# Splitting x itself for the first two pairs of weight units, and a re-planned order of taps, in a convolution and retention trunk

## The chip, the cores and the metric

One NeuronCore of a Trainium2 chip runs the whole program. Its engines work side by side, each through its own list of instructions in order: TensorE (PE, matrix products), VectorE (DVE), ScalarE (ACT), GpSimd (POOL) and SyncE (SP, which here only starts transfers). They wait for each other through semaphores. The metric is device time in microseconds (us), lower is better. A difference is called faster or slower here when it is over 0.2%, which is 1.6 us.

## The reference

Two layers over x (512 tokens by 1024), each `x <- x + Mixer(RMSNorm(x))`, and a last norm. The change lies in the first layer, a causal convolution module:

```
h = x * rsqrt(mean(x*x) + eps) * g             # per token
a, b, z = split(h @ w_in, 3)                   # 2048 columns each
u = a * sigmoid(b)
c = causal depthwise conv of u, 31 taps, + bias
mu, var = mean and variance of c over the 2048 channels
cn = (c - mu) * rsqrt(var + eps) * ln_g + ln_b
y = silu(cn) * silu(z)
x = x + y @ w_out
```

The second layer is chunked retention with its own projections. The change does not touch it.

## The kernel before, in words

x lies transposed in SBUF as 8 tiles of 128 model channels by 512 tokens. Channels of the projection are on partitions, so a per-token factor has to be a full 128x512 tile.

**Products.** A matrix product in full float32 precision is built from three faster fp32r products: each operand is split into a high part (rounded to fp32r) and a low part (the rest), and `mm3` (lines 231 to 235) adds high by high, high by low and low by high. A *unit* is 128 output columns of the weights, that is 8 blocks of k, 24 products of 128x512. Units 0 to 31 are the pairs (a_j, b_j) for j = 0 to 15, units 32 to 47 are z, and the output projection starts with unit 48. `wpack[p]` holds units 2p and 2p+1 and is loaded by SP (`load`, line 166) into a ring "raw" of two buffers. From pair 3 on, ACT casts the high part (`pos_hi`, line 202) and writes the negated high part into the low buffer (`neg_hi`, line 198), and a GpSimd DMA adds raw to it in place (`dma_lo`, line 206). Pairs 1 and 2 are split by an ACT cast (line 687) and a GpSimd subtraction (line 689).

**The head.** Pair 0 is done in the PE's slow float32 mode, straight from the loaded weights (line 328). The operand is `xg = x*g`, not yet normalised. Squares of x (line 295) are summed over channels by `token_sums` (line 288), `rsqrt` runs 11 tiny DVE operations, and `bcast_mm` (line 273) spreads the factor over the partitions as R1 in PSUM. Then for each k, `h_tile` (line 674) writes xg*R1 to PSUM, ACT casts it to the high part (line 675) and `h_lo` (line 678) makes the low part. Units 2 and 3 (lines 736, 737, 742) and all later units read these.

**The taps.** The 31 taps of each of 16 tiles u_j are shared out. DVE accumulates most of them in PSUM, one tap an instruction (line 521). ACT multiplies some into an SBUF tile (line 436), which GpSimd adds up (line 299). Some pairs of products are added by a GpSimd DMA. A planner with a clock per engine (`it`, a cost for each operation) chooses at build time what stands next on each engine: `fill` looks at what each engine could do, `pool_tile` picks the tile of the next ACT product, and `begin`, `ready` and `conv_op` run the DVE side. Tiles in `APART` keep the DVE sum and the GpSimd sum apart until a last addition (line 500). The others hand the GpSimd sum to DVE first.

**The statistics.** The LN sums run on PE: mu from the first four c tiles, `dsum` sums of c minus that mean, `st` sums of squares. Squares are added in pairs by a GpSimd DMA into `qsum` (line 625). While the last sums come in, PE works on `HOLD` z units that were kept back. Between the sums stand threes of their products. Then a factor `delta` and the new rsqrt `rs` are spread by line 273, LN is applied, and the output projection begins (line 957).

Of the kernel before, what the change touches and what calls it, by code (L numbers as in the profile page):

```python
# [45 lines left out]
SUMLATE = 1.0  # L46
# [4 lines left out]
SUMS_AT = 7  # L51
BCAST_AT = 10
# [45 lines left out]
def trunk(ctx: ExitStack, tc: tile.TileContext, xT, pos, wpack, conv_par, norms, freq, decay, out):  # L98
# [44 lines left out]
    raw0 = ring.tile([P, KD, 2, P], F32, tag="wlo", bufs=3, name="raw0")  # L143
    w0 = wpack[0].rearrange("p a (b c d) -> p (a b) c d", c=2, d=P)
    x_sb = [G() for _ in range(KD)]
    for k in range(0, KD, 2):
        (nc.scalar if k < 4 else nc.sync).dma_start(out=raw0[:, k:k + 2], in_=w0[:, k:k + 2])
        if k < 4:
            for i in range(4):
                nc.sync.dma_start(out=x_sb[2 * k + i], in_=xT[:, 2 * k + i, :])  # L150
# [163 lines left out]
    xg, sq = [], []  # L314
    pa, pb = MM(), MM()
    r1 = R1 = None
# [8 lines left out]
    nc.scalar.activation(sp.tile([P, 1], F32, name="tbl"), nrm[:, 0, 0:1], AF.Sigmoid)  # L325
    for i in range(2 * KD):
        k, c = divmod(i, 2)
        nc.tensor.matmul((pa, pb)[c], raw0[:, k, c, :], xg[k], start=k == 0, stop=k == KD - 1)  # L328
        if i == SUMS_AT:
            r1 = rsqrt(token_sums([sq[0]]), 1.0 / 1024.0)  # L330
        if i == BCAST_AT:
            R1, R1_sb = ST(), G()
            bcast_mm(r1, R1)
            nc.scalar.copy(R1_sb, R1)
    it.now = [21.7, 17.2, 17.2, 17.2, 21.0]
    it.done["R1"] = 17.2
    it.done["pab"] = 21.7
# [357 lines left out]
    h_tile(0)  # L695
    pair = split_pair(1, 17.5)
    next(pair)
    h_tile(1)
    h_lo(0)
    next(pair)  # L700
    h_tile(2)
    h_lo(1)
    list(pair)
    load(3)
    pair = split_pair(2, 21.4)
    it.run(DVE_, 0.66, lambda: nc.vector.tensor_tensor(out=sg0, in0=pb, in1=R1_sb, op=ALU.mult), "bR", ["pab"])
    it.run(ACT_, 0.52, lambda: nc.scalar.activation(sg0, sg0, AF.Sigmoid), "sg", ["bR"])
    h_lo(2)
    h_tile(3)
    it.run(DVE_, 0.66, lambda: nc.vector.tensor_tensor(out=sg0, in0=sg0, in1=R1, op=ALU.mult), "sR0", ["sg"])  # L710
    it.run(DVE_, 0.66, lambda: nc.vector.tensor_tensor(out=u0[:, PADW:], in0=pa, in1=sg0, op=ALU.mult), "u0", ["sR0"])
    u_sb[0] = u0
    h_lo(3)
    next(pair)
    h_tile(4)
    first_tap(0)
    next(pair)
    h_tile(5)
    h_lo(4)
    list(pair)  # L720
    h_tile(6)
    h_lo(5)
    h_tile(7)
    h_lo(6)
    h_lo(7)
    it.now[ACT_] = max(it.now[ACT_], 31.5)
    neg_hi(3)
    dma_lo(3)
    load(4)
# [85 lines left out]
    whi(48)  # L815
# [40 lines left out]
    whi(49)  # L856
    wlo(48, nc.gpsimd)
# [459 lines left out]
```

## Time and profile before

| what | value |
|---|---|
| median of 3 runs | 804.29 us (804.20 to 805.13) |
| the profiled execution, its own time | 804.36 us |
| its span in the profile | 802.4 us |
| PE busy | 98% of the span |
| DVE busy | 72% |
| ACT, POOL busy | 53%, 46% |
| unit 4, the first product of the normal rhythm | starts at 41.25 us |
| spread of `delta` on PE | starts at 289.94 us |

The profiled execution is 0.07 us above the median of the runs, and 1.96 us of its time lie around the span. Times in the profile are counted from the start of the span. A busy PE is not a PE at its peak: its clock can be granted at half.

### The profile page before, as it was taken

The numbers are of one execution on the slowest core, as the hardware profiler recorded it, in microseconds if no ns is written. First come the engines' busy times: TensorE is split into PE (matmuls) and PEld (weight loads), VectorE is DVE, ScalarE is ACT, GpSimd is POOL, SyncE is SP. The second block draws the span as 40 slices with busy tenths as digits, with TensorE's granted clock in tenths as the row PEclk, the third lists the DMA queues.
The fourth block names the chain that finished last, engine by engine and source line by source line (L and its number), as shares of the span: only waits on it lengthen the run. The fifth ranks groups of instructions, "written<-read, shape, count | busy, mean of one in ns | idle before, by whom it ended". The sixth has DMA issues, their size and how long they took to land.

```text
span 802.4 us, 9733 instructions
## 1 busy us (share of the span) xinstructions
PE 789.1 (98%) x3681; PEld 651.7 (81%) x3681; DVE 576.8 (72%) x855; ACT 422.2 (53%) x561; POOL 365.8 (46%) x286
## 2 busy tenths in 40 slices
PE   8999999999999999999999999999999999999995
PEld 3588888888888888888888888888888888888895
DVE  4899999999999948899574576486586467542434
ACT  3589889888998727543233413423424424332421
POOL 0578999989999848720330322340340120000300
PEclk9999999999999999999999999999999999999998
DMA  7367857897798734433213212112122212222103
GB/s 276 124 174 176 210 164 167 211 238 176 199 232 214 182 108 145 171 105 106 105 54 128 81 53 105 53 54 105 52 69 96 99 53 105 105 105 105 53 1 105
DMA packets 18958, 101.58 MB, mean 127 GB/s; under 512 B 2272, under 2 KB 4320, under 8 KB 8032
## 3 DMA queue, kind: packets, MB, share of 16 engines
q1 hardware_dynamic: 14448, 74.73, 26.6%
q0 software_dynamic: 4032, 25.69, 15.8%
q8 instruction: 29, 0.48, 0.2%
q10 hardware_dynamic: 432, 0.54, 0.2%
q14 instruction: 17, 0.14, 0.0%
HBM read 73.17 MB, written 2.10 MB: 94 GB/s over the span
## 4 chain that ended last, share of the span: by engine, by line
PE 95%; DVE 2%; DMA 2%; ACT 1%; issue 0%; SPq 0%; DVEq 0%; ACTq 0%
PE mm L233 28%; PE mm L235 27%; PE mm L234 27%; PE mm L959 2%; PE mm L957 2%; PE mm L958 2%; DMA g<-xT 1%; PE dsum L288 1%; PE mm L328 1%; PE st L288 1%; PE acc L235 1%; PE acc L234 1%; PE acc L233 1%; PE mm L742 0%; PE st L647 0%; DMA nrm<-norms 0%
## 5 line engine op out<-in xcount | busy, mean ns | idle before, releaser
L233 PE MATMUL mm<-g,whi 128*128 128x512 f32 (+1 forms) x832 | 319.8, 385 | 0.0
L234 PE MATMUL mm<-g,whi 128*128 128x512 f32 (+1 forms) x832 | 317.5, 382 | 0.0
L235 PE MATMUL mm<-g,wlo 128*128 128x512 f32 (+1 forms) x832 | 316.8, 381 | 0.0
L521 DVE SCALAR_TENSOR_TENSOR acc<-u,cpar,acc 128x512 f32<-128x512 f32 x324 | 220.8, 753 | 4.7 <-ACT acc L473 3.0
L299 POOL TENSOR_TENSOR accp<-accp,prod 128x512 f32<-128x512 f32 x142 | 190.6, 1383 | 17.2 <-ACT prod L436 10.7
L233 PEld LDWEIGHTS mm<-g,whi 128*128 128x128 f32 x832 | 156.5, 188 | 30.3 <-issue 0.7
L234 PEld LDWEIGHTS mm<-g,whi 128*128 128x128 f32 x832 | 156.5, 188 | 30.1 <-issue 1.0
L235 PEld LDWEIGHTS mm<-g,wlo 128*128 128x128 f32 x832 | 156.4, 188 | 29.9
L187 ACT CAST whi<-raw 128x1024 fp32r<-128x1024 f32 x80 | 80.7, 1050 | 111.3 <-PE mm L234 69.2
L192 DVE TENSOR_TENSOR wlo<-raw,whi 128x1024 fp32r<-128x1024 f32 x70 | 94.5, 1384 | 41.3 <-ACT whi L187 41.3
L299 POOL TENSOR_TENSOR g<-g,g 128x512 f32<-128x512 f32 x23 | 35.5, 1544 | 179.9 <-ACT g L295 171.4
L436 ACT ACTIVATE prod<-u,cpar 128x512 f32<-128x512 f32 x142 | 97.3, 719 | 20.1 <-POOL accp L299 20.0
L1045 POOL TENSOR_TENSOR g<-g,g 128x512 f32<-128x512 f32 x8 | 10.4, 1294 | 142.7 <-DVE g L1043 142.7
L228 DVE TENSOR_TENSOR g<-g,g 128x512 fp32r<-128x512 f32 x36 | 29.0, 820 | 35.7 <-ACT g L227 32.2
L227 ACT CAST g<-g 128x512 fp32r<-128x512 f32 x36 | 22.4, 623 | 60.0 <-POOL g L1045 27.8
L234 PE MATMUL mm<-wlo,g 128*128 128x512 f32 x128 | 49.8, 389 | 0.0
L235 PE MATMUL mm<-whi,g 128*128 128x512 f32 x128 | 49.6, 389 | 0.0
L233 PE MATMUL mm<-whi,g 128*128 128x512 f32 x128 | 49.3, 389 | 0.0
L198 ACT ACTIVATE wlo<-raw 128x2048 fp32r<-128x2048 f32 x21 | 40.1, 1909 | 0.0
L202 ACT CAST whi<-raw 128x2048 fp32r<-128x2048 f32 x21 | 40.0, 1904 | 0.0
L1112 POOL TENSOR_TENSOR o<-o,g 128x512 f32<-128x512 f32 x16 | 27.5, 1747 | 18.2 <-DVE g L267 18.2
L192 POOL TENSOR_TENSOR wlo<-raw,whi 128x1024 fp32r<-128x1024 f32 x10 | 24.3, 2428 | 14.9 <-ACT whi L187 14.9
(207 smaller groups left out, 960.9 us busy)
## 6 DMA issues: line engine op xcount, KB each, us to landing
raw<-wpack SPq DMA_DIRECT2D x63, 1024.0 KB, 4.8
wlo<-raw POOLq DMA_DIRECT2D x21, 1024.0 KB, 8.2
g<-xT SPq DMA_DIRECT2D x16, 256.0 KB, 6.3
q<-q POOLq DMA_DIRECT2D x6, 512.0 KB, 8.0
out_dram<-xo SPq DMA_DIRECT2D x6, 256.0 KB, 2.5
dec<-decay SPq DMA_DIRECT2D x1, 1280.0 KB, 7.5
raw<-wpack ACTq DMA_DIRECT2D x2, 256.0 KB, 5.5
raw<-wpack SPq DMA_DIRECT2D x2, 256.0 KB, 5.6
```

What stands on the lines that cost most here:

```text
L187: it.run(ACT_, 0.95, lambda: nc.scalar.copy(his[p][:, i, :], raws[p][:, i, :]), f"whi{n}")
L192: it.run(e, c, lambda: eng.tensor_tensor(out=lo, in0=raws[n // 2][:, n % 2, :], in1=hi.bitcast(F32), op=ALU.subtract), f"wlo{n}", [f"whi{n}"])
L198: it.run(ACT_, 1.8, lambda: nc.scalar.activation(los[p], raws[p], AF.Copy, scale=-1.0), f"wneg{p}")
L202: it.run(ACT_, 1.8, lambda: nc.scalar.copy(his[p], raws[p]), f"whi{p}", deps)
L228: (eng or nc.vector).tensor_tensor(out=lo, in0=src, in1=hi.bitcast(F32), op=ALU.subtract)
L233: nc.tensor.matmul(o, a[0], b[0], start=first, stop=False)
L234: nc.tensor.matmul(o, a[0], b[1], start=False, stop=False)
L235: nc.tensor.matmul(o, a[1], b[0], start=False, stop=last)
L299: eng.tensor_tensor(out=a, in0=a, in1=b, op=ALU.add)
L436: at = it.run(ACT_, 0.61, lambda: nc.scalar.activation(p, u_sb[j][:, w:w + S], AF.Copy, scale=cpar[:, j, w:w + 1]), at=add_end[n_prod[0]])
L521: it.run(DVE_, cost, lambda: nc.vector.scalar_tensor_tensor(out=c_sb[j] if last else acc, in0=u_sb[j][:, w:w + S], scalar=cpar[:, j, w:w + 1],
L1112: nc.gpsimd.tensor_tensor(out=t, in0=t, in1=RO, op=ALU.mult)
```

## The change

Pair 0 is no longer computed in float32. x*g is split into xh (ACT, line 326 of the changed kernel) and xl (DVE), raw0 into hi0 (ACT, line 330) and lo0 (DVE), and pair 0 becomes 48 products of `mm3`. Units 2 and 3 use the same xh and xl, so they no longer read R1; their u tile is multiplied with R1 afterwards, twice (bR1, sR1). R1 is spread after the first 12 products of units 2 and 3. h for unit 4 on is made from x, g and R1 in one DVE operation into PSUM. A one-element GpSimd copy named "after" reads r1, so that GpSimd's subtractions for pairs 1 and 2 stand behind it. Four products and three GpSimd additions of tile 0 are written by hand between the h tiles. In the planner, some constants change: three units are held, sums are placed with a margin of 1.5 us behind the time that the planner has for their operand, u_0 is no longer apart, pairs of tiles 4, 5 and 6 (j = 8 to 13) are added by DMA in place of 2 to 5, and the weights of the output projection are split behind the last statistics.

```diff
-PAIRS = (2, 3, 4, 5)
+PAIRS = (4, 5, 6)
-APART = (0, 1) + tuple(range(SPLIT, KI))
-POOL_CAP = 16
-LEAD = 8
-RATE = 1.6
+APART = (1,) + tuple(range(SPLIT, KI))
+POOL_CAP = 13
+LEAD = 10
+RATE = 1.69
-HOLD = 2
+HOLD = 3
-SUMLATE = 1.0
+SUMLATE = 1.5
...
-    raw0 = ring.tile([P, KD, 2, P], F32, tag="wlo", bufs=3, name="raw0")
+    raw0, hi0, lo0 = [ring.tile([P, KD, 2, P], dt, tag=tag, bufs=n, name=tag + "0")
+                      for tag, dt, n in (("raw", F32, 2), ("whi", F32R, 2), ("wlo", F32R, 3))]
...
+    def pair0(k):
+        for c, o in enumerate((pa, pb)):
+            mm3(o, (hi0[:, k, c, :], lo0[:, k, c, :]), xs[k], k == 0, k == KD - 1)
...
     for k in range(KD):
-        t = G()
-        nc.vector.tensor_scalar(out=t, in0=x_sb[k], scalar1=nrm[:, 0, k:k + 1], scalar2=None, op0=ALU.mult)
-        xg.append(t)
-        sq.append(square(x_sb[k]))
+        xh, xl = G(F32R), G(F32R)
+        g = nrm[:, 0, k:k + 1]
+        nc.scalar.activation(xh, x_sb[k], AF.Copy, scale=g)
+        if k == 0:
+            sq.append(square(x_sb[0]))
+        elif k % 2:
+            nc.scalar.copy(hi0[:, k - 1:k + 1], raw0[:, k - 1:k + 1])
+        nc.vector.scalar_tensor_tensor(out=xl, in0=x_sb[k], scalar=g, in1=xh.bitcast(F32), op0=ALU.mult,
+                                       op1=ALU.subtract)
+        if k % 2:
+            nc.vector.tensor_tensor(out=lo0[:, k - 1:k + 1], in0=raw0[:, k - 1:k + 1],
+                                    in1=hi0[:, k - 1:k + 1].bitcast(F32), op=ALU.subtract)
+        xs.append((xh, xl))
         if k:
+            sq.append(square(x_sb[k]))
             tadd(nc.vector, sq[0], sq[k])
...
+        if k % 2:
+            pair0(k - 1)
+            pair0(k)
+        if k == 1:
+            keep_warm(4)
+    token_sums([sq[0]], o_st)
+    r1 = rsqrt(o_st, 1.0 / 1024.0)
+    nc.gpsimd.tensor_copy(sp.tile([P, 1], F32, name="after"), r1[:, 0:1])
...
-        if j:
+        if j == 1:
+            it.run(DVE_, 0.66, lambda: nc.vector.tensor_tensor(out=sg, in0=pb, in1=R1_sb, op=ALU.mult), "bR1", ["mm3"])
+            it.run(ACT_, 0.5, lambda: nc.scalar.activation(sg, sg, AF.Sigmoid), "sg1", ["bR1"])
+            fill(it.done["sg1"])
+            it.run(DVE_, 0.66, lambda: nc.vector.tensor_tensor(out=sg, in0=sg, in1=R1, op=ALU.mult), "sR1", ["sg1"])
...
-        it.run(DVE_, 0.64, lambda: nc.vector.tensor_tensor(out=h_ps[k], in0=xg[k], in1=R1, op=ALU.mult), f"h{k}", ["R1"])
+        it.run(DVE_, 0.64, lambda: nc.vector.scalar_tensor_tensor(
+            out=h_ps[k], in0=x_sb[k], scalar=nrm[:, 0, k:k + 1], in1=R1, op0=ALU.mult, op1=ALU.mult), f"h{k}", ["R1"])
...
+                nc.tensor.matmul(os_[c], a, xs[k][0], start=k == 0, stop=False)
+                nc.tensor.matmul(os_[c], a, xs[k][1], start=False, stop=False)
...
+        if k == 2:
+            it.run(PE_, 0.95, lambda: bcast_mm(r1, R1), "R1", at=21.8)
```

On PE, at the end of pair 0, the order before is this (`g` under L736 is h, split; `st` under L273 is R1):

```order
L273 MATMUL st_223<-ident,rs_207 128x128 x4
L328 MATMUL mm_150<-g_175,raw_87 128x512
L328 MATMUL mm_149<-g_180,raw_87 128x512
L328 MATMUL mm_150<-g_180,raw_87 128x512
L328 MATMUL mm_149<-g_185,raw_87 128x512
L328 MATMUL mm_150<-g_185,raw_87 128x512
L736 MATMUL mm_236<-g_239,whi_244 128x512
```

and that of the changed kernel is this, at the same place (`g` under L721 is xh, under L722 xl):

```order
L235 MATMUL mm_154<-g_251,wlo_89 128x512
L288 MATMUL st_155<-ones_118,g_159 128x1 x4
L721 MATMUL mm_294<-g_156,whi_299 128x512
L722 MATMUL mm_294<-g_157,whi_299 128x512
L721 MATMUL mm_295<-g_156,whi_299 128x512
L722 MATMUL mm_295<-g_157,whi_299 128x512
```

Before, R1 was spread in the middle of pair 0 and the products of units 2 and 3 read its h. Now the sums stand behind all of pair 0, the products of units 2 and 3 follow at once, and the spread stands 12 products later.

On ACT, around the end of the h tiles, the order before is this (L675 is the high part of h, L198 the negated high part of pair 3's weights, `wlo_307`):

```order
L381 ACTIVATE accp_283<-u_124,cpar 128x512
L687 CAST whi_275<-raw_137 128x1024
L675 CAST g_287<-mm_289 128x512
L675 CAST g_294<-acc_296 128x512
L675 CAST g_300<-acc_302 128x512
L198 ACTIVATE wlo_307<-raw_262 128x2048
L661 ACTIVATE sg_360<-mm_237 128x512
L436 ACTIVATE prod_372<-u_124,cpar 128x512
```

In the changed kernel it is this (L692 is the high part of h, L448 a product of tile 0, L673 the sigmoid for u_1):

```order
L448 ACTIVATE prod_398<-u_128,cpar 128x512
L692 CAST g_400<-acc_402 128x512
L448 ACTIVATE prod_405<-u_128,cpar 128x512
L692 CAST g_408<-mm_410 128x512
L448 ACTIVATE prod_414<-u_128,cpar 128x512
L692 CAST g_416<-acc_418 128x512
L692 CAST g_422<-acc_424 128x512
L198 ACTIVATE wlo_431<-raw_305 128x2048
L673 ACTIVATE sg_439<-sg_439 128x512
```

Pair 3's negated high part stands behind the last h tile in both, but four products of tile 0 now stand between the h tiles.

On PE, at the last statistics, the order before ends like this (`q_1198` is qsum, `q_2516` the last two squares, L273 the spread of delta):

```order
L235 MATMUL mm_2561<-g_239,wlo_2417 128x512
L288 MATMUL st_1143<-ones_114,q_1198 128x1 x4
L233 MATMUL mm_2561<-g_247,whi_2471 128x512
L234 MATMUL mm_2561<-g_248,whi_2471 128x512
L235 MATMUL mm_2561<-g_247,wlo_2417 128x512
L288 MATMUL st_1143<-ones_114,q_1198 128x1 x4
L233 MATMUL mm_2561<-g_255,whi_2471 128x512
L234 MATMUL mm_2561<-g_256,whi_2471 128x512
L235 MATMUL mm_2561<-g_255,wlo_2417 128x512
L288 MATMUL st_1143<-ones_114,q_2516 128x1 x8
L273 MATMUL acc_2604<-ident,delta 128x128 x4
```

and that of the changed kernel like this (`q_1335` is qsum, `q_2592` the squares of the last two tiles, `g_2545` the last c):

```order
L288 MATMUL st_1181<-ones_118,q_1335 128x1 x4
L233 MATMUL mm_2552<-g_422,whi_2393 128x512
L234 MATMUL mm_2552<-g_423,whi_2393 128x512
L235 MATMUL mm_2552<-g_422,wlo_2346 128x512
L288 MATMUL st_1181<-ones_118,q_1335 128x1 x4
L233 MATMUL mm_2553<-g_360,whi_2499 128x512
L234 MATMUL mm_2553<-g_361,whi_2499 128x512
L235 MATMUL mm_2553<-g_360,wlo_2444 128x512
L288 MATMUL st_1181<-ones_118,q_2592 128x1 x4
L288 MATMUL dsum_1182<-ones_118,g_2545 128x1 x4
L273 MATMUL acc_2657<-ident,delta 128x128 x4
```

The sum of the last c now stands last, directly ahead of the spread of delta, and before the spread six fewer products of held units stand in the program (they stand behind it).

## Rows read from the trace of the kernel before

**Rows 1.** The page: the chain that ended last, share of the span by engine.

```profile
PE 95%; DVE 2%; DMA 2%; ACT 1%; issue 0%; SPq 0%; DVEq 0%; ACTq 0%
```

**Rows 2.** The chain of waits, 0 to 42 us: start, duration, what.

```profile
14.65 1.02 PE st L288 x8
15.67 4.38 PE mm L328 x6
20.05 0.89 PE st L273 x8
...
37.60 3.65 PE mm L742 x16
41.25 0.23 PE mm L233
```

**Rows 3.** Windows: us, then PE, PEld, DVE, ACT, POOL busy, PEclk, DMA share, GB/s.

```profile
12.83:14.62 1.79, 0.00 (x0) 0.00 (x1) 1.67 (x4) 1.20 (x2) 0.00 (x0) 1.00 0.96 387
...
15.50:19.60 4.10, 4.10 (x8) 1.80 (x8) 1.81 (x11) 0.00 (x0) 0.00 (x0) 0.58 0.56 236
...
24.60:33.20 8.60, 6.80 (x23) 3.71 (x21) 7.47 (x13) 6.58 (x10) 7.65 (x4) 1.00 0.35 122
33.20:36.60 3.40, 3.38 (x8) 2.73 (x9) 3.22 (x5) 2.40 (x2) 1.30 (x2) 0.50 0.31 75
...
35.03:279.46 244.43, 244.43 (x1111) 202.15 (x1110) 239.11 (x358) 210.82 (x260) 221.84 (x182) 1.00 0.79 197
```

**Rows 4.** Timelines of ACT, DVE and POOL, 7 to 42 us.

```profile
8.09 0.63 ACT L295 ACTIVATE g<-g 128x512 f32<-128x512 f32 x1 [2.29 <-DMA g<-xT]
9.15 3.38 ACT L295 ACTIVATE g<-g 128x512 f32<-128x512 f32 x5 [0.43 <-DMA g<-xT]
...
34.28 1.92 ACT L198 ACTIVATE wlo<-raw 128x2048 fp32r<-128x2048 f32 x1
...
17.70 0.16 DVE L267 SCALAR_TENSOR_TENSOR rs<-rs,rs 128x4 f32<-128x4 f32 x1
...
33.67 1.44 DVE L678 TENSOR_TENSOR g<-acc,g 128x512 fp32r<-128x512 f32 x2
...
35.89 6.30 DVE L521 SCALAR_TENSOR_TENSOR acc<-u,cpar,acc 128x512 f32<-128x512 f32 x8
...
23.95 7.26 POOL L689 TENSOR_TENSOR wlo<-raw,whi 128x1024 fp32r<-128x1024 f32 x3 [21.45 <-ACT whi L687]
...
36.52 1.01 POOL L206 DMA_DIRECT2D wlo<-raw  x1 [2.10 <-ACT wlo L198]
```

**Rows 5.** DMA landings: L206 all 21, L206's first, L625's last.

```profile
DMA to landing us min/median/max: 6.9/8.2/11.5
...
DMA to landing us min/median/max: 9.0/9.0/9.0
...
DMA to landing us min/median/max: 8.1/8.1/8.1
```

**Rows 6.** Groups by line: count, busy us, mean ns, idle before.

```profile
L521 DVE SCALAR_TENSOR_TENSOR acc<-u,cpar,acc 128x512 f32<-128x512 f32 x324 | 220.8, 753 | 4.7 <-ACT acc L473 3.0
L299 POOL TENSOR_TENSOR accp<-accp,prod 128x512 f32<-128x512 f32 x142 | 190.6, 1383 | 17.2 <-ACT prod L436 10.7
...
L975 DVE SCALAR_TENSOR_TENSOR g<-g,nrm,g 128x512 fp32r<-128x512 f32 x8 | 11.0, 1395 | 0.0
```

**Rows 7.** Timelines of DVE, POOL and PE, 267 to 290 us.

```profile
267.32 2.72 DVE L521 SCALAR_TENSOR_TENSOR acc<-u,cpar,acc 128x512 f32<-128x512 f32 x4
...
278.77 0.69 DVE L500 TENSOR_TENSOR g<-accp,acc 128x512 f32<-128x512 f32 x1 [0.18 <-POOL accp L299]
...
276.54 0.87 POOL L625 DMA_DIRECT2D q<-q  x1
...
285.04 0.95 PE L288 MATMUL st<-ones,q 128*128 128x1 f32 x8
...
289.94 1.14 PE L273 MATMUL acc<-ident,delta 128*128 128x128 f32 x8
```

More of the change, by code (lines that the diff above doesn't have):

```diff
@@ L147, in trunk @@
         (nc.scalar if k < 4 else nc.sync).dma_start(out=raw0[:, k:k + 2], in_=w0[:, k:k + 2])
-        if k < 4:
-            for i in range(4):
-                nc.sync.dma_start(out=x_sb[2 * k + i], in_=xT[:, 2 * k + i, :])
+        for i in range(2):
+            nc.sync.dma_start(out=x_sb[k + i], in_=xT[:, k + i, :])
+    nc.scalar.activation(sp.tile([P, 1], F32, name="tbl"), wz[:, 0:1], AF.Sigmoid)
     cpar = const.tile([P, KI, W + 3], F32, name="cpar")
@@ L313, in trunk @@
         nc.gpsimd.memset(u[:, 0:PADW], 0.0)
-    xg, sq = [], []
+    xs, sq = [], []
     pa, pb = MM(), MM()
-    r1 = R1 = None
+    o_st = ST(NT)
+    def pair0(k):
+        for c, o in enumerate((pa, pb)):
+            mm3(o, (hi0[:, k, c, :], lo0[:, k, c, :]), xs[k], k == 0, k == KD - 1)
     for k in range(KD):
-        t = G()
-        nc.vector.tensor_scalar(out=t, in0=x_sb[k], scalar1=nrm[:, 0, k:k + 1], scalar2=None, op0=ALU.mult)
-        xg.append(t)
-        sq.append(square(x_sb[k]))
+        xh, xl = G(F32R), G(F32R)
[11 more added lines that the diff above has]
+        xs.append((xh, xl))
         if k:
+            sq.append(square(x_sb[k]))
             tadd(nc.vector, sq[0], sq[k])
[L325 to L337, printed above, removed]
+        if k % 2:
[6 more added lines that the diff above has]
+    nc.gpsimd.tensor_copy(sp.tile([P, 1], F32, name="after"), r1[:, 0:1])
+    it.now = [19.6, 16.7, 21.7, 21.9, 20.0]
+    it.done["pab"] = 18.6
     c_sb = [None] * KI
@@ L442, in pool_add @@
         j, p, at = adds.popleft()
-        cost = 1.42 if acc_at[j] == it.now[POOL_] else 1.32
+        cost = 1.48 if acc_at[j] == it.now[POOL_] else 1.38
         acc_at[j] = it.run(POOL_, cost, lambda: tadd(nc.gpsimd, acc_sb[j], p), at=max(at, acc_at[j]))
@@ L694, in trunk @@
     u0, sg0 = u_ring[0], cp.tile([P, S], F32, tag="sg", bufs=1, name="sg0")
[L695 to L703, printed above, removed]
-    load(3)
[L705 to L729, printed above, removed]
+    R1, R1_sb = ST(), G()
+    list(split_pair(1, 16.7))
+    load(3)
     ws = [unit(n) for n in (2, 3)]
@@ L735, in hi_mms @@
             def hi_mms():
-                nc.tensor.matmul(os_[c], a, h_s[k][0], start=k == 0, stop=False)
-                nc.tensor.matmul(os_[c], a, h_s[k][1], start=False, stop=False)
-            it.run(PE_, 0.45, hi_mms, None, [f"hl{k}"])
+                nc.tensor.matmul(os_[c], a, xs[k][0], start=k == 0, stop=False)
+                nc.tensor.matmul(os_[c], a, xs[k][1], start=False, stop=False)
+            it.run(PE_, 0.45, hi_mms, None, ["whi1"])
+        if k == 2:
+            it.run(PE_, 0.95, lambda: bcast_mm(r1, R1), "R1", at=21.8)
     for k in range(KD):
         for c in range(2):
-            it.run(PE_, 0.227, lambda: nc.tensor.matmul(os_[c], ws[c][1][:, k * P:(k + 1) * P], h_s[k][0], start=False,
+            it.run(PE_, 0.227, lambda: nc.tensor.matmul(os_[c], ws[c][1][:, k * P:(k + 1) * P], xs[k][0], start=False,
                                                        stop=k == KD - 1), f"mm{2 + c}", ["wlo1"])
+    it.run(ACT_, 0.52, lambda: nc.scalar.copy(R1_sb, R1), "R1_sb", ["R1"])
+    h_tile(0)
+    pair = split_pair(2, 20.5)
+    next(pair)
+    it.run(DVE_, 0.66, lambda: nc.vector.tensor_tensor(out=sg0, in0=pb, in1=R1_sb, op=ALU.mult), "bR", ["pab", "R1_sb"])
+    it.run(ACT_, 0.52, lambda: nc.scalar.activation(sg0, sg0, AF.Sigmoid), "sg", ["bR"])
+    h_tile(1)
+    it.run(DVE_, 0.66, lambda: nc.vector.tensor_tensor(out=sg0, in0=sg0, in1=R1, op=ALU.mult), "sR0", ["sg"])
+    it.run(DVE_, 0.66, lambda: nc.vector.tensor_tensor(out=u0[:, PADW:], in0=pa, in1=sg0, op=ALU.mult), "u0", ["sR0"])
+    u_sb[0] = u0
+    next(pair)
+    first_tap(0)
+    product(0)
+    h_lo(0)
+    h_tile(2)
+    list(pair)
+    h_lo(1)
+    pool_add()
+    h_tile(3)
+    h_lo(2)
+    product(0)
+    h_tile(4)
+    product(0)
+    h_lo(3)
+    h_tile(5)
+    h_lo(4)
+    product(0)
+    h_tile(6)
+    h_lo(5)
+    h_tile(7)
+    pool_add()
+    pool_add()
+    h_lo(6)
+    h_lo(7)
+    it.now[ACT_] = max(it.now[ACT_], 27.0)
+    neg_hi(3)
+    fill(it.done["wneg3"])
+    dma_lo(3)
+    load(4)
+    it.now[PE_] = max(it.now[PE_], it.done["hl7"] - 4.7)
     def unit_mm(n):
```

14 lines of the change are left out of this document (6 added, 8 removed).

## The prediction

> **What bounds the kernel now.** I read the chain of waits first. 95% of the span is PE [rows 1], so time can only be won where PE waits, works at half clock, or does work that the change removes. I then looked for such places from the start. PE does pair 0 in slow float32, with the token sums in the middle of it, and unit 4 begins at 41.25 us [rows 2]. The windows show two half-clock stretches in that head: 15.5 to 19.6 us has a granted clock of 0.58, right after PE stood idle from 12.83 to 14.62, and 33.2 to 36.6 us has 0.50, after a stretch in which PE was busy for 6.8 of 8.6 us [rows 3]. From 35 to 279 us PE is busy all the time at full clock [rows 3]. So the head can be shortened, and whatever is won there is kept only if nothing later makes PE wait.
>
> Two things later could. One is DVE: from 35.03 to 279.46 us it is busy for 239.1 of 244.4 us [rows 3], and the last statistics hang on its last c, which ends at 279.46 [rows 7]. The other is the first low part made by DMA (pair 3): its transfer is issued at 36.52 and lands 9.0 us later [rows 4, 5], at 45.5. Unit 6 reads it with its third product. A product takes 3.65/16 = 0.228 us [rows 2], so that is 41.25 + 50 x 0.228 = 52.65: 7.1 us to spare before.
>
> **The head, step by step.** x's third tile is there at 8.1 [rows 4]; x and raw0 come in another order, but no tile later than the squares need. ACT then has 15 operations for k = 2 to 7 (6 xh, 6 squares, 3 casts). Five squares took 3.38 us, waits for x included [rows 4], so at most 0.68 each; I take 0.57, an estimate, which ends at 16.7. DVE has 15 too (6 xl, 3 lo0, 6 additions) and starts at about 8.9, behind the first xh of these. xl is not in the trace. The nearest operation is the tap, 0.66 us from one to the next (2.72 us for four, the last 0.75 long) [rows 7]; a two-input subtraction takes 0.72 at most [rows 4]. The same form with SBUF inputs and GpSimd at work takes 1.395 [rows 6]. GpSimd rests here, so I take 0.62, with bounds 0.58 and 1.395. The last lo0 is the 14th: 8.9 + 14 x 0.62 = 17.6. PE then has 10 products left, 2.3 us, and ends pair 0 at 19.9.
>
> Then the sums, 1.0 us [rows 2], to 20.9. rsqrt took from 15.67 to 17.86 [rows 2, 4], 2.2 us, so r1 is there at 23.1. PE fills that time with 12 products of units 2 and 3, to 23.7, and spreads R1 in 0.9 [rows 2]: **R1 at 24.6, against 20.94 before, 3.7 later.** GpSimd's rest costs nothing: its subtractions start at 23.1 in place of 23.95, at 2.4 us each [rows 4], and pair 1's low part is there at 28, ahead of its first use at 24.6 + 20 x 0.228 = 29.2. Units 2 and 3 end 36 products after the spread, at 32.8.
>
> The eight h tiles take as long as before: from R1 to the end of the last low part 35.11 - 20.94 = 14.2 us [rows 2, 4], so 38.8. h now reads x and R1 in one operation, which saves xg (8 operations) and adds nothing here; the four products between the h tiles lie in ACT's idle time. PE is through units 2 and 3 by 32.8, so unit 4 follows the low parts and ends one block after the last, at about 39.3. Unit 5 ends at 44.8, and unit 6's third product comes at 45.3.
>
> **What is late next: pair 3's low part.** Its negation stands on ACT behind the last h tile, as before, and R1 is 3.7 later. From R1 to the DMA's issue it was 36.52 - 20.94 = 15.6 us [rows 2, 4], so the issue comes at 40.2. The 21 transfers of this kind take 6.9 to 11.5 us, the first 9.0 [rows 5]. That first one ran beside the load of pair 4, which starts when GpSimd has split pair 2. In the changed kernel GpSimd ends that at about 33, and the load is over by 40, so I take the lower bound: 47.1, with 49.2 above. PE waits 1.8 us there. By the Trainium skill ("DMA: Bandwidth & Descriptors", section on the SWDGE path) a transfer on this path costs about 2.0 us plus its bytes at 436 GB/s, which is an estimate of 4.4 us for 1 MB. The trace disagrees: none of 21 took less than 6.9 us [rows 5].
>
> So at unit 6's third product PE leads by 52.65 - 47.1 = 5.5 us. An idle 1.79 us stood before the first half-clock stretch of the trace [rows 3], and the wait here is as long, so I count on a third such stretch: 3.4 us at 0.50 [rows 3] loses 1.7. **The lead is then 3.8 us.** The skill's page "TensorE: Matmul & The Clock Gate" (section on HAM oscillation) shows a kernel whose waits between bursts of products bring the lower rate each time. By that the 1.7 is lost, without it the lead is 5.5.
>
> **The tail.** DVE starts its taps later: R1 + 14.2, and then u_1 needs a product with R1, a sigmoid behind pair 3's negation, another product and u itself, 2.8 us: 41.6 in place of 35.03. But it has less to do. In the two orders I count 3 taps fewer (2.3 us at 0.753 [rows 6]), 17 fewer taps directly behind one of the same sum (0.79 from one to the next within such a row [rows 4], 0.66 in alternation [rows 7], so 2.2 us), one last addition and one u tile fewer (0.7 each). That is 5.8, so 239.1 - 5.8 = 233.3 us of work. It waited 5.3 us in that stretch before. GpSimd now starts adding within the head and has 9 additions fewer (12 us [rows 6]) for 6 more short DMA issues, so I take 3.5, with 2 and 5.3 as bounds. **The last c ends at 41.6 + 233.3 + 3.5 = 278.4** (276.9 to 280.2), against 279.46.
>
> The last DMA of squares stands ahead of five GpSimd additions of 1.38 us [rows 6], so it is issued 8.2 to 9.5 us before the last c and lands 8.1 later [rows 5], 0.1 to 1.4 us before it. From the first sum that reads it to the spread of delta it was 289.94 - 285.04 = 4.9 us [rows 7]; the new order has the same pieces there. So DVE and the DMA allow the spread at 278.4 + 3.7 to 5.0 = 282.1 to 283.4. PE gets there by its own work at 289.94 - 3.8 - 1.4 = 284.7, where 1.4 is the six products that now stand behind the spread, so that the time is not won by them. PE is the later one, so the whole lead arrives. Behind the spread PE has 36 products in place of 30 to cover the rsqrt and the LN, and the moved casts and subtractions of the output weights (2.4 us each on GpSimd [rows 4]) lie under these. All this is priced at nothing.
>
> **Sum.** 804.36 (the profiled execution, 0.07 above the median) - 3.8 = 800.5 us; against the median I say **800.4**.
>
> **The rivals.** *The full lead.* Pair 3's low part lands in time (R1 by 23, or h tiles faster). Then unit 6 leads by 7.3 us, no clock falls, and the tail caps the gain at 288.5 - 282.8 = 5.7: about 798.5. For it speaks that the first h tile can be ready as soon as R1 is; against it that the negation is behind all h tiles on ACT.
>
> *DVE is the bound.* If its waits grow instead of shrinking, say 4 us more, the last c ends at 282.4, the spread comes at 287.0 and the gain is 1.5: 802.9, no measurable change. For it: DVE has 98% of that stretch full, and its taps start 6.6 us later. It decides from a last c of about 281. A half-clock stretch in pair 0, which has waits after every 12 products, would delay R1 by up to 2.3 us and lead to the same time.
>
> *Slower.* The 15 DVE operations of the head cost what L975 does. Each 0.1 us more delays R1 by 1.5. The gain is gone at 0.62 + 3.8/15 = 0.87 us each, and at 0.98 the kernel is 0.2% slower; at 1.1 it takes 807.9. For it: xl reads two SBUF tiles, and the only row of this form says 1.395 [rows 6]. Against it: GpSimd was busy in those rows and rests here. The Trainium skill ("GPSIMD Engine Reference", key points) says that GpSimd and VectorE contend for SBUF when a VectorE instruction has two SBUF inputs; no run here shows xl alone.
>
> *The rest does nothing.* The head's copy that holds GpSimd back changes no time if GpSimd would not start before r1 anyway; this is inside the first case.
>
> **How the numbers follow.** Chances: forecast 0.52 (798.7 to 802.6, from the lead of 5.5 without the clock's fall to a landing at 49.2 with it, partly hidden), full lead 0.2, DVE bound or a slow pair 0 0.16, slower 0.12. The first two are faster by over 0.2% (that is 1.6 us, about what a measurement can tell), 0.71 with their upper edge taken off; the third is the same, 0.17 with that edge. The range of 797.4 to 804.6 leaves out most of the slower case and the far end of the full lead.
>
> **What would show it.** Right: the spread of R1 at 24 to 25 us; xl near 0.7; units 2 and 3 without a wait; unit 6's third product waiting for the DMA of pair 3 until about 47, and a clock below 1 behind it; last c at 277 to 280; the spread of delta at 284 to 286. Wrong: R1 after 27, xl above 1 us, PE waits between 50 and 270 us that before did not have (for u, for low parts), or a last sum that waits for the DMA of squares beyond 286.

## The result

The changed kernel takes 807.36 us at the median of 13 runs (803.13 to 814.36), the kernel before 803.79 us at the median of 13 on the same chip in the same rounds (800.52 to 807.62). The ratio is 1.0056 (95% interval 1.0036 to 1.0077): **slower by 0.56%**, where 800.4 us was forecast. The profiled execution took 807.09 us with a span of 805.3 us, 2.9 us more than before.

The head came out as forecast. First the timelines of DVE, PE, POOL and ACT, 14 to 40 us, then a piece of PE's timeline at 46 us:

```profile
15.51 0.75 DVE L331 SCALAR_TENSOR_TENSOR g<-g,nrm,g 128x512 fp32r<-128x512 f32 x1
...
22.99 1.05 PE L273 MATMUL st<-ident,rs 128*128 128x128 f32 x8
...
22.66 9.52 POOL L706 TENSOR_TENSOR wlo<-raw,whi 128x1024 fp32r<-128x1024 f32 x4
39.30 1.01 POOL L206 DMA_DIRECT2D wlo<-raw  x1 [1.76 <-ACT wlo L198]
...
37.06 1.92 ACT L198 ACTIVATE wlo<-raw 128x2048 fp32r<-128x2048 f32 x1
...
46.43 0.65 PE L235 MATMUL mm<-g,wlo 128*128 128x512 f32 x1 [1.83 <-DMA wlo<-raw]
```

xl takes 0.75 us. R1 is spread from 22.99 to 24.0 (forecast 23.7 to 24.6), pair 3's DMA is issued at 39.30 (40.2) and lands at 46.39 (47.1), and unit 6 waits 1.83 us for it (1.8). Before, the same product ran at 52.4, so PE leads by 6.0 us (5.5).

Next the waits of DVE and of PE, 35 to 300 us (who waits for what: us in total, times, longest), and windows (columns as in [rows 3]):

```profile
DVE acc L533 <- ACT acc L485: 6.5, 3, 5.2
DVE delta L892 <- PE dsum L288: 2.9, 1, 2.9
DVE u L679 <- ACT sg L677: 2.8, 1, 2.8
DVE sg L675 <- ACT sg L673: 1.0, 1, 1.0
...
PE mm L235 <- DMA wlo<-raw: 1.8, 1, 1.8
PE dsum L288 <- DVE g L512: 1.5, 1, 1.5
```

```profile
40.98:285.76 244.78, 241.21 (x1093) 198.34 (x1092) 233.92 (x352) 206.47 (x258) 209.55 (x174) 0.99 0.85 208
...
46.40:50.00 3.60, 3.57 (x9) 2.80 (x10) 3.60 (x6) 3.60 (x5) 2.43 (x3) 0.53 1.15 218
...
274.50:280.00 5.50, 5.47 (x20) 4.27 (x20) 5.08 (x8) 4.45 (x8) 5.34 (x5) 0.69 0.82 252
...
288.00:292.00 4.00, 3.75 (x18) 3.37 (x18) 2.98 (x13) 0.50 (x2) 1.78 (x1) 0.62 0.44 136
```

From its first tap (40.98) to the last c (285.76) DVE is busy for 233.9 us, as forecast (233.3), but idle for 10.9 us (forecast 3.5). So the last c is 7.4 us later than forecast. PE then waits 1.5 us for a c, and there are two half-clock stretches (1.2 in place of 2.4 GHz) in the tail that the kernel before did not have in its profile. The end of the tail, DVE and PE:

```profile
285.07 0.69 DVE L512 TENSOR_TENSOR g<-accp,acc 128x512 f32<-128x512 f32 x1
...
274.53 1.18 PE L288 MATMUL dsum<-ones,g 128*128 128x1 f32 x8 [1.50 <-DVE g L512]
...
288.82 1.97 PE L273 MATMUL acc<-ident,delta 128*128 128x128 f32 x8 [0.26 <-DVE delta L892]
...
302.61 0.58 PE L984 MATMUL mm<-g,whi 128*128 128x512 f32 x1
```

The first product of the output projection stands at 302.6, against 300.7 before. Unit 44 still began 4.9 us ahead (265.8 against 270.7). From there PE lost 2.0 us to waits and 3.2 to the two stretches ((1 - 0.69) x 5.5 and (1 - 0.62) x 4), and did one sum more, 0.8; the remaining 0.7 I can't place. The last 1.0 of the 2.9 us lies behind 302 us.

Where the longest wait comes from, by the chain of waits of the changed kernel, 150 to 187 us, and the landing times of the pair additions, the low parts and the loads of weights:

```profile
155.51 1.82 ACT wlo L198
157.33 0.29 issue
157.62 14.20 DMA wlo<-raw
171.82 0.02 SPq L168
171.84 0.03 issue
171.87 11.12 DMA raw<-wpack
...
183.07 0.04 ACT wlo L198
183.11 1.78 issue
184.89 0.59 ACT acc L485
185.48 0.02 issue
185.50 2.07 DVE acc L533 x3
```

```profile
DMA to landing us min/median/max: 4.5/6.4/11.9
...
DMA to landing us min/median/max: 6.9/7.4/14.2
...
DMA to landing us min/median/max: 4.7/4.8/11.1
```

A low part takes 14.2 us to land (longest before 11.5 [rows 5]). The load behind it needs its buffer, starts at 171.9 and takes 11.1 us (median 4.8; longest before 10.0). ACT stands at that pair's negation for 5.7 us, the copy that hands a GpSimd sum to DVE (L485) stands behind it on ACT, and DVE waits 5.15 us for the copy. In that time two of seven pair additions (512 KB each) are on their way, issued at 156 and 171 us.

### The profile page after: what moved, and what is told of

The parts are those of the page before. It is cut to its first block, busy times and chain, and to the rows that moved or that the text cites. A ratio compares the mean times of both kernels' runs of the same rounds, so it can differ in the third digit from the quotient of the medians.

```text
span 805.3 us, 9796 instructions
## 1 busy us (share of the span) xinstructions
PE 790.8 (98%) x3701; PEld 656.9 (82%) x3701; DVE 579.0 (72%) x857; ACT 428.2 (53%) x576; POOL 359.8 (45%) x284
## 4 chain that ended last, share of the span: by engine, by line
PE 63%; DVE 16%; ACT 6%; DMA 5%; issue 5%; POOL 5%; DVEq 0%; POOLq 0%; ACTq 0%; SPq 0%
PE mm L233 18%; PE mm L234 18%; PE mm L235 18%; DVE acc L533 14%; POOL accp L299 3%; DMA wlo<-raw 3%; DMA raw<-wpack 2%; PE mm L986 2%; PE mm L985 2%; PE mm L984 2%; ACT prod L448 2%; ACT wlo L198 1%; POOL wlo L706 1%; ACT whi L202 1%; PE acc L235 1%
## 5 line engine op out<-in xcount | busy, mean ns | idle before, releaser
L233 PE MATMUL mm<-g,whi 128*128 128x512 f32 (+1 forms) x848 | 328.6, 388 | 0.8 <-ACT whi L330 0.8
L235 PE MATMUL mm<-g,wlo 128*128 128x512 f32 (+1 forms) x848 | 324.8, 384 | 2.1 <-DMA wlo<-raw 1.8
L234 PE MATMUL mm<-g,whi 128*128 128x512 f32 (+1 forms) x848 | 325.4, 384 | 0.4 <-DVE g L695 0.3
L533 DVE SCALAR_TENSOR_TENSOR acc<-u,cpar,acc 128x512 f32<-128x512 f32 x321 | 216.9, 753 | 8.0 <-ACT acc L485 6.5
L235 PEld LDWEIGHTS mm<-g,wlo 128*128 128x128 f32 x848 | 160.3, 189 | 34.5 <-DMA wlo<-raw 2.4
L233 PEld LDWEIGHTS mm<-g,whi 128*128 128x128 f32 x848 | 160.6, 189 | 32.8 <-ACT whi L330 1.7
L234 PEld LDWEIGHTS mm<-g,whi 128*128 128x128 f32 x848 | 160.7, 190 | 32.0 <-DVE g L695 1.4
L299 POOL TENSOR_TENSOR accp<-accp,prod 128x512 f32<-128x512 f32 x133 | 179.9, 1411 | 13.9 <-ACT prod L448 8.4
L448 ACT ACTIVATE prod<-u,cpar 128x512 f32<-128x512 f32 x133 | 91.2, 716 | 16.7 <-POOL accp L299 16.5
L1072 POOL TENSOR_TENSOR g<-g,g 128x512 f32<-128x512 f32 x8 | 10.4, 1296 | 142.4 <-DVE g L1070 142.4
L198 ACT ACTIVATE wlo<-raw 128x2048 fp32r<-128x2048 f32 x21 | 40.1, 1908 | 10.5 <-DMA raw<-wpack 10.5
```

The source lines that it names most:

```text
L198: it.run(ACT_, 1.8, lambda: nc.scalar.activation(los[p], raws[p], AF.Copy, scale=-1.0), f"wneg{p}")
L233: nc.tensor.matmul(o, a[0], b[0], start=first, stop=False)
L234: nc.tensor.matmul(o, a[0], b[1], start=False, stop=False)
L235: nc.tensor.matmul(o, a[1], b[0], start=False, stop=last)
L299: eng.tensor_tensor(out=a, in0=a, in1=b, op=ALU.add)
L448: at = it.run(ACT_, 0.61, lambda: nc.scalar.activation(p, u_sb[j][:, w:w + S], AF.Copy, scale=cpar[:, j, w:w + 1]), at=add_end[n_prod[0]])
```

## The experiments

Each was compared with the kernel before, run in the same rounds. "First product" is that of the output projection in the profiled run.

**1. Small pair additions.** Nothing but the bytes of seven transfers is changed (only the call is shown):

```diff
-nc.gpsimd.dma_start(out=sums2[n], in_=p, accum_op=ALU.add)
+nc.gpsimd.dma_start(out=sums2[n][:, :, 0:16], in_=p[:, :, 0:16], accum_op=ALU.add)
```

> The same program in the same order, but the seven GpSimd DMAs that add a pair of products (512 KB each) move only 16 of 512 columns, so those products are left out of the sum. Theory A (these transfers crowd the DMA engines in the tap phase, the load of a weight pair then lands up to 11.1 us after its issue, ACT stands 5.7 us at its negation, and DVE 5.2 us at 185 us): the load at 172 us lands in 5 us, the 5.2 us wait of DVE is gone, the last c ends 5 us earlier, at about 280.5, and with it the 1.5 us wait of PE at 273 us and one or both half-clock stretches of the tail: 801 to 804 us, 0.4 to 0.8% under the changed kernel. Theory B (the time is lost at the start, by pair 3's late low part): the last c comes at most 1 us earlier, and the time stays within 0.2% of 807.4. Theory C (the order of the sums at the end makes PE wait, whatever DVE does): the last c is earlier but the half-clock stretches at 275 and 288 us stay, 805 to 807.

Measured: 802.49 us, ratio 0.9986 (0.9970 to 1.0003). DVE's waits, 35 to 300 us, then the landing of weight loads, the last c, and two windows of the tail:

```profile
DVE u L679 <- ACT sg L677: 2.7, 1, 2.7
DVE acc L533 <- ACT acc L485: 1.3, 2, 1.2
```

```profile
DMA to landing us min/median/max: 4.7/4.8/8.6
```

```profile
281.31 0.69 DVE L512 TENSOR_TENSOR g<-accp,acc 128x512 f32<-128x512 f32 x1
```

```profile
262.00:280.00 18.00, 18.00 (x97) 15.45 (x96) 17.32 (x27) 14.07 (x20) 17.30 (x15) 1.00 0.72 200
280.00:304.00 24.00, 23.75 (x123) 20.11 (x122) 13.04 (x29) 9.18 (x14) 12.98 (x9) 0.93 0.45 143
```

The wait of 5.2 us is gone and the last c ends at 282.0, 3.8 us earlier than in the changed kernel (about 5 were expected). PE waits for no c in the tail, and the first of the two half-clock stretches is gone. The second is not: the clock of 0.93 from 280 to 304 us is a loss of 1.7 us around the spread of delta. The first product comes at 299.4, 3.2 us earlier. With the order untouched, the bytes of these additions are worth 0.6 to 0.7% against the changed kernel; against the kernel before, this version is not clear of no change. Theory A holds.

**2. Pair 3's low part early.** Only ACT's and GpSimd's order changes, and only here:

```diff
     h_tile(4)
+    new_lo(3)
+    nc.scalar.activation(los[3], raws[3], AF.Copy, scale=-1.0)
+    nc.gpsimd.dma_start(out=los[3], in_=raws[3], accum_op=ALU.add)
...
-    neg_hi(3)
...
-    dma_lo(3)
```

> Pair 3's negated high part and its DMA stand behind the fifth h tile in place of the eighth, and two products of tile 0 behind the eighth; every other order is the same. Theory B: the transfer is issued at about 35.3 in place of 39.3 and lands at 42 to 44; unit 6 does not wait (1.8 us before), there is no half-clock stretch at 46.4 (1.7 us), ACT's 4.8 us wait for the load of pair 5 shrinks to at most 1, DVE's 2.8 us wait for u_2 is gone, and the last c ends about 3 us earlier; 802 to 804.5. Theory A: PE gains its 3.5 us at 50 us, but DVE still waits at 185 us, and the last c is at most 3 us earlier than 285.8, so that the gain is lost at the last sums: within 0.3% of 807.4. A third: the sums at the end then wait longer, since PE is further ahead, and the kernel is not faster at all.

Measured: 808.47 us, 1.0048 (1.0021 to 1.0074). Neither the wait at 46 us nor the half clock behind it is there, and DVE's wait for u_2 is gone. But DVE has other waits in its place and is still idle for 10.2 us from its first tap to the last c. And PE, now further ahead, waits elsewhere, as its waits show:

```profile
PE st L658 <- DVE g L533: 2.0, 1, 2.0
PE mm L235 <- DMA wlo<-raw: 1.4, 1, 1.4
```

So a lead won in the head is given back at the first sum whose c is late, and at a low part delayed by the crowd. The late low part of pair 3 is not what makes the kernel slower.

**3. No pair additions.** `PAIRS = ()`, the whole plan anew.

> PAIRS is empty: no pair of products is added by DMA, and the planner gives these products to GpSimd's additions or the taps to DVE, in a new order. Theory A: no transfer of a weight pair takes over 9 us because of them, DVE's wait at 185 us is gone, but DVE and GpSimd have up to 14 products more to share (about 4 taps at 0.66 more on DVE): last c at 281 to 284, 803 to 806. Theory B: no gain or a loss, 807 to 810, as DVE has more to do.

Measured: 801.67 us, 0.9973 (0.9962 to 0.9984), **faster than before**, and faster than either theory had it. The tail's window:

```profile
280.00:304.00 24.00, 23.75 (x134) 20.26 (x133) 17.08 (x35) 10.50 (x16) 16.76 (x12) 1.00 0.48 147
```

The longest load takes 8.6 us, the longest low part 9.6, DVE's waits before the sums add up to 6.3 us, and the first product comes at 298.0. DVE has 4 taps more and the last c ends at 284.9, only 0.9 us earlier than in the changed kernel. The first product comes 4.6 us earlier even so: PE does not wait for a c in the tail and has no half clock there. So a late last c does not cost by itself.

**4. The constants with the old head.** Two versions: the five planner constants, and the same without APART.

> The kernel before with its own head, sums and held units, and only the five planner constants of the change (PAIRS, APART, POOL_CAP, LEAD, RATE); its plan has 6 pair additions by DMA in place of 1. Theory A (the pair transfers cost): loads and low parts land later between 130 and 240 us, DVE waits 3 us or more longer there than before, and the time is 0 to 0.6% over the kernel before. Theory B (only the new head is at fault): the same as before within 0.2%, or faster by what DVE saves in taps (up to 0.3%).

> The kernel before with its own head and u_0 apart as it was, and the other four constants of the change (PAIRS, POOL_CAP, LEAD, RATE): 6 pair additions by DMA in place of 1. It takes out the 7.4 us wait of DVE at 42 us that the first trial with the old head had, because u_0 was no longer apart there. Theory A (the pair transfers cost by themselves): loads land late between 150 and 240 us, DVE waits 3 us or more there, and the time is 0.2 to 0.6% over before. Rival (with the old head's start the transfers are hidden): within 0.2% of before, or faster through 25 fewer taps on DVE (up to 0.5%).

Measured: 809.50 us, 1.0070 (1.0049 to 1.0092), and 807.01 us, 1.0052 (1.0032 to 1.0072). In the first, DVE stands idle for 7.4 us at 42 us, since u_0 is no longer apart there and DVE must first take up GpSimd's sum. DVE's waits, 30 to 300 us:

```profile
DVE acc L521 <- ACT acc L473: 10.9, 7, 7.4
```

In the second this wait is gone, loads take up to 12.3 us and low parts up to 12.9. Its profiled execution is the fastest of its seven (804.12 us) and does not show the loss. The constants lose with the old head too.

**5. The old constants with the new head.**

> The changed kernel with the five planner constants of before (PAIRS, APART, POOL_CAP, LEAD, RATE); head, margins for sums and three held units stay. Its plan has 3 pair additions by DMA in place of 7, and u_0 apart. Theory A: fewer transfers, so DVE's wait at 185 us is under 3 us and the time lies between the run with no pairs and the changed kernel, 802 to 805. If it is the head that costs, and not the constants, it is 807 or more.

Measured: 803.78 us, 1.0007 (0.9987 to 1.0027): no difference to before, and 0.5% under the changed kernel. Its three pair additions land in at most 5.1 us. The head is not what costs. Together with run 4: the new constants cost 0.5% with either head (1.0052 and 1.0056), and the new head with its sums and held units neither gains nor loses anything measurable by itself (1.0007).

**6. Both cures.** Early pair 3 with small additions, and early pair 3 with none.

> Both edits at once: pair 3's negation behind the fifth h tile, and the seven pair additions moving 16 of 512 columns (those products are left out of the sum), every other order kept. Theory A with B behind it (the pair transfers are the main loss, the late low part the second): neither the wait at 46 us (1.8 us) with its half-clock stretch (1.7) nor DVE's waits at 61.7 (2.7) and 185 us (5.2) are there; last c at 278 to 280, the first product of the output projection at 296 to 297; 798.5 to 800.5. Rival (PE is ahead of DVE whatever is done to pair 3, so that the lead is spent at the next sum, as PE's 2.0 us wait at 86 us in the run with the early low part alone): no faster than the run with small pair transfers alone, 801.5 to 803.

> The whole computation, with no pair additions by DMA and the early pair 3; its plan is that of the run with no pairs, except for pair 3 on ACT and GpSimd. By theory A with B behind it: 2 to 3.5 us faster than the run with no pairs (801.7), 798 to 799.7. By the rival (the lead is spent at the mu sums near 86 us): within 1 us of 801.7.

Measured: 801.68 us, 0.9977 (0.9956 to 0.9999), about what the small additions give alone, so the rival has it there; and **800.13 us, 0.9950 (0.9928 to 0.9973)**, the fastest version. It lies between its two expectations, and its gain over run 3 (0.9973) is not clear of the intervals. The latter's windows and the waits of DVE, 30 to 285 us:

```profile
41.00:60.00 19.00, 19.00 (x86) 15.73 (x85) 18.72 (x29) 17.21 (x20) 13.49 (x12) 1.00 0.77 187
...
280.00:304.00 24.00, 23.63 (x120) 19.72 (x119) 15.70 (x33) 10.60 (x16) 15.31 (x10) 0.93 0.47 143
```

```profile
DVE acc L533 <- ACT acc L485: 2.4, 2, 2.3
DVE sg L675 <- ACT sg L673: 0.7, 1, 0.7
```

The first product comes at 297.6, 3.1 us earlier than before; DVE's waits are down to 4.2 us.

**7. GpSimd not held back.** The one-element copy is left out.

> The changed kernel without the one-element copy that holds GpSimd back until r1. GpSimd then starts pair 1's subtractions at about 16.7, while DVE does its last subtractions and additions of the head and rsqrt. What the prediction says: R1 moves by under 0.3 us, pair 1's low part is ready 5 us earlier and waits, and the time is the same within 0.2%. Rival (GpSimd slows DVE's two-input operations in the head, as 0.69 against 1.39 us would have it): the last two or three of them take 1.4 us, R1 comes 1 to 2 us later, and the time is 0.1 to 0.3% longer.

Measured: 813.29 us, 1.0118 (1.0091 to 1.0145): the largest loss of all, and not by the way that I had as a rival. DVE and POOL, 17 to 24 us:

```profile
17.91 0.68 DVE L299 TENSOR_TENSOR g<-g,g 128x512 f32<-128x512 f32 x1
...
21.62 1.58 DVE L255 TENSOR_SCALAR rs<-rs 128x4 int32<-128x4 int32 x1
...
17.86 5.32 POOL L705 TENSOR_TENSOR wlo<-raw,whi 128x1024 fp32r<-128x1024 f32 x2 [15.36 <-ACT whi L703]
```

The two-input addition at 17.9 is not slowed. GpSimd's two subtractions beside it take 5.32 us, the first two of the changed kernel 4.77, so there it may be GpSimd that waited. But a tiny operation of rsqrt takes 1.58 us in place of 0.17, and ends when GpSimd's subtraction ends, at 23.2. That is 1.4 us on the way to R1; the sums ahead of it came 1.1 us later in this execution too. The last c ends 2.0 us later, and the tail runs at half clock from 285 to 299 us. The Trainium skill ("SBUF — State Buffer", "SBUF: two separate sides") calls the port pair that VectorE shares with GpSimd an exclusive lock held for a whole instruction; this trace agrees in this operation.

The changed kernel's own profile has a second case, behind the spread of delta. DVE's operation ends at 289.80, GpSimd's subtraction at 289.78:

```profile
288.80 1.00 DVE L894 SCALAR_TENSOR_TENSOR var<-delta 128x4 f32<-128x4 f32 x1
...
287.43 2.35 POOL L192 TENSOR_TENSOR wlo<-raw,whi 128x1024 fp32r<-128x1024 f32 x1 [3.26 <-ACT whi L187]
```

In the kernel before, the same operation takes 0.16 us. It cost nothing here, as PE reached the spread of rs by its own work.

**8. The tail's clock.** The changed kernel's 13 runs have mean granted clocks from 0.998 (803.1 us) to 0.982 (814.4 us). Four kernels look for the reason: two of the pair additions small; more products between the last sums; idle products ahead of the sum of c 13, for which PE waits; and the same ahead of the first sum of squares as well.

```diff
-GAP = 0.6
+GAP = 1.3
```

```diff
+        if which and tile is c_sb[13]:
+            for _ in range(7):
+                nc.tensor.matmul(idle, wz[:, 0:P], wz, start=True, stop=True)
```

> The changed kernel in its own order; only the second and the third of the seven pair additions, issued at 156 and 171 us, move 16 of 512 columns (those products are left out of the sum). Theory A in its narrow form: these two are the ones that met a load and a low part (10.7 and 11.9 us to land, the load at 172 us 11.1), so the 5.2 us wait of DVE at 185 us goes with them alone; last c at about 281 to 282 and the time of the run with all seven small, 802 to 803.5. If the crowding is that of all seven, the wait shrinks by half at most or shows up at another load, and the time is 804.5 to 807.

> The changed kernel, its orders on ACT, DVE and GpSimd untouched, with six products of held units between the last sums on PE in place of three (GAP 1.3 for 0.6). Theory D (PE's clock falls to half where PE waits for a c and then works through sums with little between them; in the worst runs it stays there for 13 us): the products lie between the sums, the wait at 274.5 us is 0.8 us shorter, the granted clock from 274 to 292 us is 0.9 or more, and no run has a mean clock under 0.988: 802.5 to 806. Rival (it is the late last c itself that costs, wherever the products stand): the spread of delta comes no earlier, and the time stays within 0.2% of the changed kernel, 806 to 809.

> The changed kernel with seven idle products (on zeros, 0.2 us each) ahead of the sum of c 13, where PE waits 1.5 us for DVE. Nothing else is moved, and no useful work is gained. Theory D: the wait is filled, the half-clock stretch behind it at 274.5 to 279 us (1.7 us) does not come, the later sums run at full clock more often, and the median falls by 2 to 4 us, to 803 to 805.5. Rival (the wait costs only what it lasts): the same as the changed kernel within 0.2%, or 0.5 us slower where the filler is longer than the wait.

> The changed kernel with seven idle products ahead of the sum of c 13 and seven more ahead of the first sum of squares, to which PE's wait moved when only the first place was filled (1.5 us at 280.8 us, with 13.7 us of half clock from 284 us). Theory D (a wait right ahead of the thin stretch of sums brings the half clock): both waits are filled, PE is never idle from 270 us to the spread of delta, the stretch of 13.7 us does not come, and the median is 803 to 806. Rival (the thin sums bring it by themselves): half clock behind 284 us in most runs as before, mean clock 0.987 or lower, 809 to 813.

Measured, in this order: 811.19 (1.0069, 1.0037 to 1.0101), 810.21 (1.0068, 1.0041 to 1.0096), 811.68 (1.0095, 1.0061 to 1.0129) and 807.55 us (1.0064, 1.0039 to 1.0089). No expected time was met. In the first, the wait at 185 us is gone, but other loads land late (up to 10.4 us, low parts 12.3), so it is not those two transfers alone; and its runs lie from 802 us at a clock of 0.998 to 813 at 0.984. In the second, the profiled run has no half clock in the tail, but PE waits 3.6 us for two low parts that took 11.0 and 12.7 us. In the third, the wait only moved to the next sum. PE's timeline there, and two windows:

```profile
280.81 1.05 PE L288 MATMUL st<-ones,q 128*128 128x1 f32 x8 [1.48 <-ACT q L628]
```

```profile
280.00:284.00 4.00, 3.19 (x22) 2.97 (x23) 3.82 (x7) 1.30 (x3) 3.77 (x4) 1.00 0.27 53
284.00:298.00 14.00, 13.75 (x55) 12.51 (x54) 6.09 (x20) 2.82 (x4) 4.02 (x3) 0.51 0.19 57
```

From 3 us behind that wait on, 14 us pass at half clock, while PE does sums with three products between. With both waits filled, all six runs have a clock of 0.991 or more, but the idle products themselves take 3.0 us.

These two runs alone would say that the wait ahead of the sums brings the long stretch. Two other readings of the traces speak against it. In the profiled run with both waits filled, the clock still falls: PE is busy without a break from 270 to 288 us, and then its products take 0.63 us each in place of 0.39 until 295 us. And run 7 has the same 14 us at half clock (from 285 us) behind a wait of only 0.25 us. Its wait of 1.45 us lies at 275 us and has a half-clock stretch of its own, from 278.5 to 282 us. PE's timelines, first with both waits filled, then in run 7:

```profile
292.12 0.63 PE L235 MATMUL mm<-g,wlo 128*128 128x512 f32 x1
```

```profile
282.26 1.05 PE L288 MATMUL st<-ones,q 128*128 128x1 f32 x8 [0.25 <-ACT q L627]
```

In run 5, on the other hand, PE waited 1.1 us ahead of its first sum of squares and ran at 1.00 from 280 to 304 us. So what brings the long stretch, and why some executions of one program have it and others not, stays open.

**9. The fastest version with more products between the last sums.**

> The fastest version so far (early pair 3, no pair additions by DMA, 800.1) with six products between the last sums in place of three. If thin sums are what is left of the half clock there (3.4 us at 287 us), 798.5 to 800. If the later spread of delta takes back what the clock gives, 800 to 802.

Measured: 800.33 us, 0.9970 (0.9958 to 0.9982), with a clock of 0.995 to 0.999 in 12 runs: steadier, not faster.

**10. Two held units.** No pairs, `HOLD = 2`.

> The run with no pairs (801.7, 0.27% under before) with two z units held in place of three; its end is planned anew. If the third held unit is what pays for the later last c (it ended at 284.9 there, 5 us later than before, and the time was still shorter), PE waits for the last sums or runs idle products for 3 to 5 us and the time is 804 to 807. Rival (the held unit makes no difference, since the sums stand where c is ready): within 0.2% of 801.7.

Measured: 802.35 us, 0.9982 (0.9967 to 0.9997), first product at 297.6. The third held unit is worth nothing measurable here.

**11. A wider margin for sums.** The fastest version with `SUMLATE = 3.0`.

> The early pair 3 and no pairs (800.1), with the margin behind the planned end of c for every sum raised from 1.5 to 3.0 us. If PE's lead over the plan is what makes it wait at the mu sums (0.8 us at 84.7 us, and a granted clock below 1 behind such waits), this wait is gone and the clock higher: 797.5 to 799.5. If the later sums only move the wait to the end (the last sums and the spread of delta later), 800 to 803.

Measured: 802.68 us, 1.0013 (0.9986 to 1.0039). The wait at the mu sums is gone, but the 12 runs spread from 798.6 (clock 0.998) to 809.2 us (0.983). Inconclusive: the best run is as fast as the best of the version with the old margin (798.7), the median is not.

## Why the prediction was wrong

**The head: right.** R1, xl, units 2 and 3 without a wait, pair 3's low part, its wait of 1.8 us and the half clock behind it came within 1 us of their places. The executions scatter by as much: with the same head, the first tap comes 0.9 us later in runs 1 and 3.

**DVE's work: right** (233.9 against 233.3 us), and so was the start of its taps (40.98 against 41.6).

**DVE's waits: the step that failed.** The term "for 6 more short DMA issues, so I take 3.5" measured 10.9. The additions by DMA (seven, one in the kernel before) were priced at their issue on GpSimd, and their bytes at nothing. They share the DMA engines with loads and low parts, and these were already on a tight cycle: a load waits for the buffer that a low part frees, ACT waits in order for the load, DVE for ACT. The profile before showed it: 79% of the DMA engines' time was used from 35 to 279 us [rows 3], and low parts took up to 11.5 us [rows 5]. Seven additions made it 85%; with the small ones it is 79% again (run 1, 41 to 282 us). Of the 10.9 us, 6.1 are left with the small additions (run 1), 10.2 with pair 3 early and the additions whole (run 2), and 4.3 with both (run 6). So the bytes are the larger part, and pair 3's place shows only once they are gone.

**GpSimd's rest: priced at nothing, worth 1.4 us** ahead of R1 (run 7). That run is 0.6% slower than the changed kernel, but how much of it is the rest's doing is not settled: kernels with the same head as the changed one went to 1.0095 (run 8).

**The tail: "PE is the later one, so the whole lead arrives" fell with it.** The rival "DVE is the bound" came about in part. By its chain a last c at 285.8, for 282.4 in its example, would put the spread of delta at 290.4 and the loss at 1.9 us. The spread came at 288.8, only 3.1 us behind the last c. What took the lead is that PE waited for an earlier c (1.5 of 2.0 us of waits in the tail) and worked at half clock (3.2 us in the profiled run, more in others), which neither the forecast nor the rival had there. Of the 3.2 us, 1.7 lie behind the wait for that c and go with it (run 1). The other 1.5, around the spread of delta, stand in a like size in run 1, where PE waits for no c, and what brings them is open. Of the signs that the prediction set, those of the head came; the last c (277 to 280) and the spread (284 to 286) were late, and no sign of it looked at waits of PE for a c behind 270 us.

The clock is not the whole loss. The changed kernel's two runs at a mean clock of 0.998 took 803.1 and 803.5 us. Six runs of the kernel before at that clock, in the rounds of the experiments, took 800.7 to 801.6. So about 2 us stand without it. The rest goes with the clock, which is 0.989 at the median of the changed kernel's runs and 0.995 at that of the kernel before.

**Rivals that fell.** The head's DVE operations cost 0.75 and 0.69 us, or 0.60 to 0.66 from one start to the next (0.62 in the sum), far from 1.395. One addition beside a GpSimd subtraction took 0.68 (run 7). The full lead of the first rival was reached in run 2, and was worth nothing as long as DVE was late.

**Small slips in its sums.** The savings of DVE (2.3, 2.2, 0.7 and 0.7) add up to 5.9 us, not 5.8. The spread could follow the last c by 3.5 to 4.8 us, not 3.7 to 5.0. At 1.1 us for each operation of the head its rule gives 807.7 us, not 807.9. None of them bears on the result.

## What to carry to other kernels

Price a transfer by what it shares: when its bytes meet loads that an in-order engine waits for, a cheap issue can cost several times itself two engines further on. A lead won at the start is worth what the slowest later stage lets through, so read that stage's waits first. Where one engine must finish a chain of tiny operations, keep long instructions of the engine that shares its port away from it.

## What was not expected of the hardware

- A 0.17 us VectorE operation on 128x4 elements took 1.58 us, until a GpSimd subtraction of 128x1024 ended (run 7), and another took 1.00 in place of 0.16 in the changed kernel. A two-input addition of 128x512 beside the same kind of subtraction took 0.68.
- One program's time follows its granted clock: 803.1 us at 0.998, 814.4 at 0.982. The long stretch of the profiles (14 us at 0.51, runs 7 and 8) lies where PE does 128x1 sums with three products between. Such sums also ran at 1.00 (run 3, 280 to 304 us). Waits ahead of them were 1.48 and 0.25 us in the two profiles that have the long stretch, and 1.1 us in one that has none (run 5).
